# Pacing the first loads of the down projection at one per unit, starting them in the last gate/up block and holding that block's two pairs back

## The chip, the cores and the metric

One core of one Trainium2 chip runs the whole kernel. The metric is the device time of one execution in microseconds (us); times are medians of several runs, and one further execution of the kernel was profiled.

## What is computed

The reference is one decoder layer on 512 tokens of 2048 channels: a norm, three token mixers side by side, an output projection and a residual, then a norm and a SwiGLU feed-forward part with a residual:

```python
x = x + mix @ w_out[l]
h2 = _rms_norm(x, norm2_g[l])
x = x + (jax.nn.silu(h2 @ w_gate[l]) * (h2 @ w_up[l])) @ w_down[l]
```

The hidden width of the feed-forward part is 5632 = 44 tiles of 128. The change touches the two large stages of this last line: gate/up and down. Inputs and outputs are float32.

## The kernel before

**Products.** Both stages use a two-by-two block scheme with seven products in place of eight (a Strassen-like scheme), and every float32 product is made of three matmuls of rounded halves: high by high, high by low, low by high. So a weight block becomes `wh` and `wl`, and the other operand is a tile of two halves in one of 73 slots of 128 x 512 (`N_SLOTS`, L50; helper `slot`, L138).

**Units.** The work is a list of weight blocks of up to 128 x 1024. One block is one *unit*: 12 matmuls of 512 columns, or 6 for a block of half the size. For each unit the program writes down, in this order: the sums of raw weights that are due (`sums_now`, L289, GpSimd), the evacuations (`run(evacs)`), `next_unit` (L293) and the matmuls. `next_unit` asks for at most two more raw weight loads (`pump`, L235, 0.5 MB each on SP's queue at L243, eight buffers) and splits the block that is used two units later (`split_up_to`, L257: ScalarE writes `wn` at L269 and `wh` at L270, VectorE writes `wl` at L271, each from three buffers). After the matmuls come the loads of other operands (`load_next`) and the late work (`run(extras)`). Each engine works its own list in order, and waits only where a buffer or an operand is not ready; SP issues every DMA named here.

**Gate/up** (`class Up`, L1166) has 11 blocks (`NBLOCKS`) of 28 units: first four channel pairs by seven products of two units, then the other four pairs. The operands `ops[q, j]` come from the output projection; the steps of its last channel pair are still due when the first block begins, and L1324 runs one such step (`ticks.tick`) a unit: casts on ScalarE (L1030), and differences and low halves on VectorE (L1022 to L1036). When a block is done, its result (`b{n}c`, stored at L1266 into a DRAM tile `bd`) is read back turned, as two `Pair`s (L1119). A pair takes 17 extras: two reads of four 64 KB pieces (L1131), GpSimd sums (L1144 to L1149), seven pieces split by ScalarE (L1112) and GpSimd (L1116) and stored at L1101 into DRAM tiles `od`, from which the down stage reads its operands. L1241 puts the two pairs of a block at 5 and 18 extras after its end.

**Down** (`class Down`, L1361) has twelve steps t = 0 to 11, two for each of six ranges of pairs (`RANGES`: 4, 3, 4, 3, 4, 4 pairs). A step has seven products of two units, 14 units; with four pairs every unit has 12 matmuls, with three the second unit of a product has 6. I number the units of down from 0 (step t begins at unit 14t) and those of the last gate/up block from -28 to -1, and write "unit 6 of a step" for a place in it. Steps 2 and 3 work on the second range (pairs 4 to 6).

**The feed** (L1298 to L1316) is a fixed list of 170 loads of 256 KB: operands `a` (L1316) of the first range in the order of the products, mixed with the residuals `y` (L1311), of which eight belong to step 0 and eight to step 1; then the ranges that follow. I number the loads from 0: 0 to 35 belong to step 0, 36 to 43 are the residuals of step 1, 44 to 64 the operands of steps 2 and 3, 65 to 92 those of steps 4 and 5. `load_next(n, limit)` asks for the next n of them. Before the change it is asked for two in each unit of the second half of the last gate/up block (28 loads in units -14 to -1), two in each unit of step 0 (units 0 to 13), and one in each unit afterwards, as long as fewer than 46 operands are held (`FEED`).

The lines that set the pace:

```python
if n == NBLOCKS - 1 and blk.first:
    load_next(2)
...
load_next(2 if self.t == 0 else 1, FEED)
...
later(5 + 13 * at, Pair, self.dram, 2 * self.n + at, at, queue=extras)
```

Of the kernel before, what the change touches and what calls it, by code (L numbers as in the profile page):

```python
# [70 lines left out]
FEED = 46  # L71
NBLOCKS = NP // 2
# [44 lines left out]
def kernel(ctx: ExitStack, tc: tile.TileContext, xT, wi, wo, wgu, wd, cst_in, outT):  # L117
# [18 lines left out]
    ticks = Ticks()  # L136

    def slot(name, dt=F32, cols=T):  # L138
        return sp.tile([P, cols], dt, name=name, tag="s")
# [66 lines left out]
    for t, (g, r) in enumerate(DOWN):  # L206
        first, end = RANGES[r]
# [25 lines left out]
    at = {"entry": 0, "split": 0, "use": 0}  # L233
# [55 lines left out]
    def sums_now():  # L289
        for fn in sums.pop(at["use"], ()):  # L290
            fn()
# [143 lines left out]
    for k in range(KT):  # L435
# [5 lines left out]
        if k == 0:  # L441

            at["use"] = 2
            first = [splits.pop(u) for u in range(2)]
# [15 lines left out]
        if k == 0:  # L460
# [5 lines left out]
            first = w = None  # L466
# [613 lines left out]
    def norm2():  # L1080

        b = psum["high"].tile([P, 1024], F32, name="r2s", tag="h")[:, :NT]
        n2["r"] = token_scale(ssum2, D, "n2", b)[1]
# [3 lines left out]
    evacs, extras = [], []  # L1087
# [10 lines left out]
    def run(queue):  # L1098

        for fn, *args in queue.pop(0) if queue else ():  # L1100
            fn(*args)  # L1101

    def later(n, fn, *args, queue=evacs):
        while len(queue) <= n:
            queue.append([])
        queue[n].append((fn, *args))
# [59 lines left out]
    class Up:  # L1166
# [4 lines left out]
        def product(self, q):  # L1171
            banks = outs[:2]
            outs[:] = outs[2:] + banks
            for c in range(2):
                sums_now()
                run(evacs)
                wh, wl = next_unit()
                for a, b in enumerate(banks):
                    high, low = slice(a * P, (a + 1) * P), slice(TH + a * P, TH + (a + 1) * P)
                    for f in range(2):  # L1180
                        x, s = ops[q, self.first + 2 * c + f], slice(f * T, (f + 1) * T)
                        nc.tensor.matmul(b, x[:, high], wh[:, s], start=c == f == 0 and q in (7, 1, 5, 2), stop=False,  # L1182
                                         skip_group_check=True)
                        nc.tensor.matmul(b, x[:, high], wl[:, s], start=False, stop=False, skip_group_check=True)  # L1184
                        nc.tensor.matmul(b, x[:, low], wh[:, s], start=False, stop=c == f == 1, skip_group_check=True)  # L1185
                yield
                run(extras)
            later(0, self.done, self.first == 0, q, banks)
# [21 lines left out]
        def done(self, first, q, banks):  # L1210
            if first and q == 7:
                self.c = {}
            by = self.keep if first else self.add
            for a, b in enumerate(banks):
                if q == 7:
                    by(1, 1, a, b)
                elif q == 1:
                    by(0, 0, a, b)
                elif q == 4:
                    by(1, 0, a, b)  # L1220
                elif q == 6:
                    by(0, 1, a, b)
                    self.less(0, a, b)
                    self.less(1, a, b)
                elif q == 5:
                    self.less(1, a, b)
                else:
                    self.add(0, q - 2, a, b)
            if first:
                return  # L1230
            if q in (6, 5):
                later(1, self.gate, 6 - q, queue=extras)
            elif q == 2:
                self.dram = tc.dram_tile([T, T], F32, name=f"bd{self.n}")
            if q in (2, 3):
                later(0, self.weigh, q - 2)
                later(2, self.turn, q - 2)
                later(3, self.store, q - 2, queue=extras)
            if q == 3:
                for at in range(2):  # L1240
                    later(5 + 13 * at, Pair, self.dram, 2 * self.n + at, at, queue=extras)  # L1241

        def scale(self, k, a):
            i = 2 * k + a
# [41 lines left out]
    def turn_x2(key):  # L1286

        z = turns[key] = slot("z")
        for part in range(4):
            nc.sync.dma_start(by_blocks(z, part), turned(x2d, key, part))  # L1290
# [14 lines left out]
    def load_next(n, limit=99):  # L1305
        while feed and n and len(acts) < limit:
            key = feed.pop(0)
            n -= 1
            if len(key) == 4:
                y[key] = slot("y")  # L1310
                nc.sync.dma_start(y[key], x2t[key])  # L1311
            else:
                q, j = key
                acts[key] = slot(f"a{q}_{j}", F32R)
                at = LAID.index(q)
                nc.sync.dma_start(acts[key].bitcast(F32), od[j][:, at * T:(at + 1) * T])  # L1316

    for n in range(NBLOCKS):
        blk = Up(n)
        for blk.first in (0, 4):  # L1320
            for i, q in enumerate(ORDER):
                for c, _ in enumerate(blk.product(q)):
                    at_unit = (7 if blk.first else 0) * 2 + 2 * i + c
                    if ticks.due:  # L1324
                        ticks.tick()
                    if n == 0 and at_unit == 12:
                        norm2()
                    if 1 <= n <= 8 and at_unit in (9, 23):
                        key = SUMS[2 * n - 2 + at_unit // 16]
                        turn_x2(key)  # L1330
                        later(6, turn_x2_now, key)
                    if n == NBLOCKS - 1 and blk.first:
                        load_next(2)
                if n == NBLOCKS - 1:
                    for j in range(4):
                        ops.pop((q, blk.first + j))
# [24 lines left out]
    class Down:  # L1361
# [10 lines left out]
        def product(self, k, q):  # L1372
            banks = outs[:2]
            outs[:] = outs[2:] + banks
            tail = self.end and k == 6
            units = []
            for c in range(2):
                sums_now()
                run(evacs)
                units.append((next_unit(), list(enumerate(self.pairs[2 * c:2 * c + 2]))))  # L1380
                if not tail:
                    for a in range(2):
                        self.multiply(q, banks[a], units[c:], a, 0, T, c == 0, c == 1)
                    load_next(2 if self.t == 0 else 1, FEED)
                    run(extras)
            if tail:

                out = banks + outs[:1]
                sides = psum["high"].tile([P, 2, T], F32, name="sides", tag="h")
                last = [slot(f"end{c}")[:, :TH].rearrange("p (b a j) -> p b a j", a=2, j=32) for c in range(2)]  # L1390

                def turn(a):

                    src = y[self.sum(0, 1, a)]
                    for c in range(2):
                        nc.tensor.transpose(sides[:, c, a * P:(a + 1) * P], src[:, TH + c * P:TH + (c + 1) * P], ident)
                    for c in range(2):
                        eng, copy = ((nc.vector, nc.vector.tensor_copy), (nc.scalar, nc.scalar.copy))[c if a else 1]
                        copy(last[c][:, :, a], sides[:, c, a * P:(a + 1) * P].rearrange("p (b j) -> p b j", j=32))

                for n, (a, lo, hi) in enumerate(((0, 0, T), (1, 0, TH), (1, TH, T))):
                    if n == 2:
                        turn(0)
                    self.multiply(q, out[n], units, a, lo, hi, True, True)
                    if n == 0:
                        for b in range(2):
                            turn_back(self.sum(0, 0, b))
                        put(self.g, 0, 0)
                    t = y[self.sum(0, 1, a)][:, lo:hi]
                    nc.vector.tensor_add(t, t, out[n][:, lo:hi])  # L1410
                    if n < 2:
                        turn_back(self.sum(0, 1, a), 0, TH)
                    if n == 1:
                        put(self.g, 0, 1, 0, TH)
                turn(1)
                for c in range(2):
                    to = 512 * self.g + TH + c * P
                    nc.sync.dma_start(outT.rearrange("n p t -> (n p) t")[to:to + P, TH:], last[c].rearrange("p b a j -> p (b a j)"))
                return
            if self.drops:  # L1420
                for j in self.pairs:
                    acts.pop((q, j))
            later(0, self.done, q, banks)
# [64 lines left out]
    for t in range(len(DOWN)):  # L1488
        blk = Down(t)
# [87 lines left out]
```

## Time and profile before

| what | before |
|---|---|
| median of 3 runs | 1869.19 us (1866.34 to 1869.68) |
| the profiled execution's own time | 1867.57 us |
| its span, first to last instruction | 1865.7 us |
| granted TensorE clock, mean | 0.999 |
| first gate/up matmul, first and last down matmul | 581.7, 1422.4 and 1860.4 us |

The profile's page gives busy time by engine, the span in 40 slices, the chain of work that ended last, and groups of instructions. Further views give waits (who waited for whom), stretches of the span (busy time, number of instructions, granted clock and DMA share in each), and instructions in order of time. PE is TensorE, DVE VectorE, ACT ScalarE, POOL GpSimd; a trailing q is an engine's sequencer. The time between a DMA's issue and its landing is its landing time.

### The profile page before, as it was taken

Reading aid. Unit: us, or ns where it says so; the run is one execution under the profiler, and the core shown is the slowest. Engines: PE = TensorE matmul, PEld = TensorE weight load, DVE = VectorE, ACT = ScalarE, POOL = GpSimd, SP = SyncE. Lnnn points to the kernel's source line nnn. Section 1 sums busy time; section 2 is a strip of 40 time slices with the busy share of each in tenths; the row PEclk is TensorE's granted clock in tenths of the full one; section 3 lists DMA queues with packets and bytes.
Section 4 is the critical chain, followed back from the end, with each engine's and each line's share of the span. In section 5 each row is a group of like instructions: output and inputs, shape, how many; then the busy total and the mean of one; then the engine's idle time right before and its main releaser. Section 6 shows DMA issues by size and latency. Waiting matters only on the chain.

```text
span 1865.7 us, 26613 instructions
## 1 busy us (share of the span) xinstructions
PE 1844.3 (99%) x8370; PEld 1527.3 (82%) x8370; DVE 1432.0 (77%) x2052; ACT 1321.4 (71%) x1794; POOL 1103.0 (59%) x850
## 2 busy tenths in 40 slices
PE   9999999999999999999999999999999899999999
PEld 7888888888887888888888888888888677888887
DVE  6778878998689777777777777777777477777777
ACT  6355644553458788888888888878888577778775
POOL 0135533100003567777787877867877799879775
PEclk9999999999999999999999999999999999999999
DMA  7242253343343366777776876777679887566545
GB/s 273 83 140 92 77 146 97 92 131 119 133 139 107 103 164 177 206 213 177 220 196 189 220 198 185 221 183 218 175 227 285 277 269 268 197 222 234 178 140 113
DMA packets 382988, 330.36 MB, mean 177 GB/s; under 512 B 171648, under 2 KB 311552, under 8 KB 382848
## 3 DMA queue, kind: packets, MB, share of 16 engines
q1 hardware_dynamic: 382704, 328.66, 59.6%
q8 instruction: 66, 1.08, 0.2%
q14 instruction: 74, 0.61, 0.1%
q10 hardware_dynamic: 144, 0.01, 0.0%
HBM read 255.56 MB, written 64.63 MB: 172 GB/s over the span
## 4 chain that ended last, share of the span: by engine, by line
PE 92%; DMA 3%; POOL 2%; DVE 1%; issue 1%; ACT 1%; SPq 0%; POOLq 0%; DVEq 0%; ACTq 0%
PE out L1184 15%; PE out L1182 15%; PE out L1185 15%; PE out L1432 6%; PE out L1431 6%; PE out L1433 6%; PE o L310 3%; PE o L308 3%; PE o L309 3%; PE cq L308 2%; PE cq L309 2%; PE cq L310 2%; PE ak L308 1%; PE aq L308 1%; PE av L308 1%
## 5 line engine op out<-in xcount | busy, mean ns | idle before, releaser
L1184 PE MATMUL out<-wl,h 128*128 128x512 f32 x1232 | 479.4, 389 | 1.6 <-DVE wl L271 1.6
L1182 PE MATMUL out<-wh,h 128*128 128x512 f32 x1232 | 479.4, 389 | 0.0
L1185 PE MATMUL out<-wh,h 128*128 128x512 f32 x1232 | 479.3, 389 | 0.0
L1184 PEld LDWEIGHTS out<-wl,h 128*128 128x128 f32 x1232 | 231.3, 188 | 50.0 <-DVE wl L271 2.0
L1185 PEld LDWEIGHTS out<-wh,h 128*128 128x128 f32 x1232 | 231.3, 188 | 48.0
L1182 PEld LDWEIGHTS out<-wh,h 128*128 128x128 f32 x1232 | 231.3, 188 | 47.8
L1431 PE MATMUL out<-wh,a 128*128 128x512 f32 x620 | 242.0, 390 | 11.6 <-ACT wh L270 11.6
L1432 PE MATMUL out<-wl,a 128*128 128x512 f32 x620 | 242.0, 390 | 1.7 <-DVE wl L271 1.6
L1433 PE MATMUL out<-wh,a 128*128 128x512 f32 x620 | 241.1, 389 | 0.0
L275 ACT CAST wh<-w 128x1024 fp32r<-128x1024 f32 (+2 forms) x94 | 96.9, 1031 | 154.2 <-PE o L309 64.8
L1431 PEld LDWEIGHTS out<-wh,a 128*128 128x128 f32 x620 | 116.8, 188 | 39.0 <-ACT wh L270 15.1
L253 DVE TENSOR_TENSOR wl<-w,wh 128x1024 fp32r<-128x1024 f32 (+2 forms) x95 | 113.1, 1191 | 42.3 <-ACT wh L275 40.8
L1432 PEld LDWEIGHTS out<-wl,a 128*128 128x128 f32 x620 | 116.7, 188 | 27.6 <-DVE wl L271 3.3
L1433 PEld LDWEIGHTS out<-wh,a 128*128 128x128 f32 x620 | 116.9, 189 | 23.6
L1441 DVE TENSOR_TENSOR y<-y,out 128x512 f32<-128x512 f32 x164 | 106.1, 683 | 22.5 <-PE out L1433 20.8
L519 DVE SCALAR_TENSOR_TENSOR y<-bu,cst,y 128x511 f32<-128x511 f32 (+14 forms) x120 | 89.9, 749 | 0.7
L308 PE MATMUL o<-mh_c,wh 128*128 128x512 f32 x128 | 51.1, 399 | 0.0
L308 PE MATMUL cq<-hh,wh 128*128 128x512 f32 x128 | 50.5, 395 | 0.0
L310 PE MATMUL o<-mh_c,wl 128*128 128x512 f32 x128 | 50.0, 391 | 0.0
L309 PE MATMUL cq<-hl,wh 128*128 128x512 f32 x128 | 49.9, 390 | 0.0
L309 PE MATMUL o<-ml_c,wh 128*128 128x512 f32 x128 | 49.9, 390 | 0.0
L310 PE MATMUL cq<-hh,wl 128*128 128x512 f32 x128 | 49.9, 390 | 0.0
(2376 smaller groups left out, 4877.4 us busy)
## 6 DMA issues: line engine op xcount, KB each, us to landing
od<-a SPq DMA_DIRECT2D x154, 256.0 KB, 4.1
a<-od SPq DMA_DIRECT2D x154, 256.0 KB, 6.0
w<-in_wi SPq DMA_DIRECT2D x58, 512.0 KB, 3.3
w<-in_wo SPq DMA_DIRECT2D x32, 512.0 KB, 3.3
x<-in_xT SPq DMA_DIRECT2D x16, 256.0 KB, 6.9
xr<-in_xT SPq DMA_DIRECT2D x16, 256.0 KB, 3.6
x2d<-xr SPq DMA_DIRECT2D x16, 256.0 KB, 2.0
z<-x2d SPq DMA_DIRECT2D x64, 64.0 KB, 4.1
```

What stands on the lines that cost most here:

```text
L253: fn(*args)
L275: (nc.vector.tensor_copy if u == 0 else nc.scalar.copy)(hi[:, :n], t[:, :n])
L308: nc.tensor.matmul(out, wh, xh, start=start, stop=False)
L309: nc.tensor.matmul(out, wh, xl, start=False, stop=False)
L310: nc.tensor.matmul(out, wl, xh, start=False, stop=stop)
L1182: nc.tensor.matmul(b, x[:, high], wh[:, s], start=c == f == 0 and q in (7, 1, 5, 2), stop=False, skip_group_check=True)
L1184: nc.tensor.matmul(b, x[:, high], wl[:, s], start=False, stop=False, skip_group_check=True)
L1185: nc.tensor.matmul(b, x[:, low], wh[:, s], start=False, stop=c == f == 1, skip_group_check=True)
L1431: nc.tensor.matmul(b[:, lo:hi], x[:, high], wh[:, s], start=start, stop=False, skip_group_check=True)
L1432: nc.tensor.matmul(b[:, lo:hi], x[:, high], wl[:, s], start=False, stop=False, skip_group_check=True)
L1433: nc.tensor.matmul(b[:, lo:hi], x[:, low], wh[:, s], start=False, stop=last, skip_group_check=True)
L1441: getattr(eng, op)(t, t, src)
```

## The change

Three edits, in gate/up and down:

- The two pairs of the last gate/up block start 25 and 45 extras after its end, not 5 and 18.
- The feed is asked for one load a unit throughout: 24 loads in units -24 to -1 (all units of the last block but its first four), and one in each unit of step 0 as well.
- The steps of the last channel pair run in every second unit (the odd ones) of the first gate/up block.

```diff
             if q == 3:
+                first, every = (25, 20) if self.n == NBLOCKS - 1 else (5, 13)
                 for at in range(2):
-                    later(5 + 13 * at, Pair, self.dram, 2 * self.n + at, at, queue=extras)
+                    later(first + every * at, Pair, self.dram, 2 * self.n + at, at, queue=extras)
...
-                    if ticks.due:
+                    if ticks.due and at_unit % 2:
                         ticks.tick()
...
-                    if n == NBLOCKS - 1 and blk.first:
-                        load_next(2)
+                    if n == NBLOCKS - 1 and at_unit > 3:
+                        load_next(1)
...
-                    load_next(2 if self.t == 0 else 1, FEED)
+                    load_next(1, FEED)
```

## The prediction

> **What bounds the kernel now.** The page comes first. TensorE is the bound, and the chain of work that ended last is 92% PE, so only TensorE's idle time can be gained.
>
> ```profile
> span 1865.7 us, 26613 instructions
> PE 1844.3 (99%) x8370; PEld 1527.3 (82%) x8370; DVE 1432.0 (77%) x2052; ACT 1321.4 (71%) x1794; POOL 1103.0 (59%) x850
> ...
> PE 92%; DMA 3%; POOL 2%; DVE 1%; issue 1%; ACT 1%; SPq 0%; POOLq 0%; DVEq 0%; ACTq 0%
> ```
>
> The view by stretches shows where it idles. The numbers after x are matmuls: 443 in an undisturbed 100 us, one per 0.227 us.
>
> ```profile
> 500.00:600.00 100.00, 98.39 (x435) 81.17 (x434) 84.21 (x142) 65.99 (x120) 15.18 (x7) 1.00 0.38 126
> ...
> 1400.00:1500.00 100.00, 90.93 (x384) 72.17 (x383) 64.33 (x76) 70.96 (x89) 73.55 (x54) 0.98 0.88 281
> 1500.00:1600.00 100.00, 95.74 (x419) 78.00 (x418) 72.34 (x91) 75.49 (x98) 92.46 (x66) 1.00 0.81 267
> 1600.00:1700.00 100.00, 100.00 (x443) 82.84 (x442) 74.22 (x93) 75.09 (x92) 78.14 (x49) 1.00 0.63 204
> ```
>
> 59 + 24 matmuls are missing after 1400, that is 83 x 0.227 = **18.8 us**, and 8 before 600, **1.8 us**: 20.6 us to be had. The waits of PE name who ended them, and the order in time shows the worst.
>
> ```profile
> PE out L1431 <- ACT wh L270: 11.6, 8, 2.7
> PE out L1184 <- DVE wl L271: 1.6, 1, 1.6
> PE out L1432 <- DVE wl L271: 1.6, 3, 0.7
> ```
>
> ```profile
> 1467.26 0.50 PE L1431 MATMUL out<-wh,a 128*128 128x512 f32 x1 [2.73 <-ACT wh L270]
> ...
> 1469.24 0.63 PE L1431 MATMUL out<-wh,a 128*128 128x512 f32 x1
> 1469.67 0.63 PE L1432 MATMUL out<-wl,a 128*128 128x512 f32 x1
> ...
> 1491.88 0.50 PE L1431 MATMUL out<-wh,a 128*128 128x512 f32 x1 [1.72 <-ACT wh L270]
> ...
> 1545.79 0.50 PE L1431 MATMUL out<-wh,a 128*128 128x512 f32 x1 [1.42 <-ACT wh L270]
> ```
>
> After the idle time of 2.73 us matmuls start 0.43 us apart, not 0.227, for eight of them: a second price of about 1.65 us. After 1.72 us idle nothing of the kind shows. So an idle time of 2.7 us costs 4.4.
>
> Why was `wh` late? SP, POOL and ACT in order of time, before that first long wait (unit 15):
>
> ```profile
> 1453.27 4.55 SPq L1131 DMA_DIRECT2D p20l<-bd  x4
> 1457.93 1.44 SPq L243 DMA_DIRECT2D w('11', 'd1B')_14171<-in_wd  x1
> ```
>
> ```profile
> 1462.81 2.38 POOL L172 TENSOR_TENSOR w('s', 'd1B')_14277<-w('21', 'd1B')_14137,w('11', 'd1B')_14171 128x1024 f32<-128x1024 f32 x1 [4.73 <-DMA w('11', 'd1B')_14171<-in_wd]
> ```
>
> ```profile
> 1465.22 1.02 ACT L269 CAST wn<-w('s', 'd1B')_14277 128x1024 fp32r<-128x1024 f32 x1 [5.10 <-POOL w('s', 'd1B')_14277 L172]
> ```
>
> The weight was asked for only at 1457.93, behind the reads of pair 20, and POOL then idled 4.73 us for it. The DMA side was full there: the second half of the last gate/up block, step 0, and for comparison step 6 of down (the last two numbers are DMA share and GB/s).
>
> ```profile
> 1384.30:1422.40 38.10, 38.10 (x170) 31.56 (x169) 28.71 (x32) 32.09 (x39) 25.73 (x20) 1.00 0.93 284
> 1422.40:1460.90 38.50, 37.97 (x166) 30.66 (x165) 27.22 (x32) 27.67 (x34) 31.92 (x24) 1.00 0.89 301
> 1650.70:1679.30 28.60, 28.60 (x128) 23.68 (x127) 22.64 (x30) 21.82 (x30) 22.66 (x15) 1.00 0.66 208
> ```
>
> **The change part by part.** *Steps of the last channel pair.* The short stall near 594 is VectorE's: the low halves and differences of that pair stand in front of a `wl`, and one of them takes 2.63 us.
>
> ```profile
> 587.95 2.63 DVE L1036 TENSOR_TENSOR h<-tb,h 128x256 fp32r<-128x256 f32 x1
> ...
> 593.35 1.21 DVE L271 TENSOR_TENSOR wl<-w('22', 'u0A')_5725,wn 128x1024 fp32r<-128x1024 f32 x1
> ```
>
> Four steps are left when gate/up begins; they go from units 0 to 3 to units 1, 3, 5 and 7. Their results are read from unit 14 on and the sum of squares at unit 12, so nothing waits for them. I take the whole 1.8 us; the bounds are 0 and 1.8.
>
> *Fewer loads in step 0, pairs moved.* Step 0 loses 14 loads of 256 KB (3.7 MB of the 11.6 MB that 38.5 us at 301 GB/s make) and steps 0 and 1 lose the reads of pairs 20 and 21, so the rate falls to some 205 GB/s, that of step 6, which has no stall. In units -14 to -1 the same 14 loads go. Ten loads appear in units -24 to -15, 2.6 MB in 27 us, hidden by weights that come two units ahead; bounds 0 and 1. What stays is POOL's work in step 0:
>
> ```profile
> 1427.59 0.74 POOL L1144 TENSOR_TENSOR p19a<-p19l 128x256 f32<-128x256 f32 x1
> ...
> 1432.29 2.54 POOL L1257 TENSOR_TENSOR b10c<-b10c,b10c 128x512 f32<-128x512 f32 x2
> ...
> 1439.50 1.43 POOL L1116 TENSOR_TENSOR a<-p19r,a 128x256 fp32r<-128x256 f32 x2
> ...
> 1442.99 2.56 POOL L1441 TENSOR_TENSOR y<-y,d0u 128x512 f32<-128x512 f32 x2
> ```
>
> Eight weight sums of 2.4 us (19.2), four products of the last block (5.1), pair 19 with four sums of 0.74 and seven pieces of 0.72 (8.0) and eight residual sums of 1.28 (10.2) are 42.5 us for a step of 38. The small waits of step 0 (before 1467) are its share; I leave 0.8 us. **Saved: 18.8 + 1.8 - 0.8 = 19.8 us.**
>
> *What is late next: the loads themselves.* This is the term that decides. At one a unit the feed runs close to its use. By unit 28, where step 2 begins, 24 + 28 = 52 loads have been asked for: the 44 of steps 0 and 1 and 8 of step 2. Step 2 eats three in two units and gets two. So its last loads are asked for hardly ahead: with full units of 2.72 us and half ones of 1.36, load 55 is asked for 8.2 us before its matmul, 58 6.8, 59 5.4, 60 4.8, 61 4.1, 62 4.1, 63 2.0 and 64 2.7 us. In step 0 load 35 has 6.1 us, in step 4 loads 90 to 92 have 6.1, 5.4 and 3.4 us.
>
> How long does a load take from its unit's start? Step 6 has the same half units and one load a unit. It begins with the matmul at 1650.71, so its units 3 to 12 start at 1657.5, 1658.9, 1661.6, 1663.0, 1665.7, 1667.0, 1669.8, 1671.1, 1673.8 and 1675.2.
>
> ```profile
> 1650.71 0.39 PE L1431 MATMUL out<-wh,a 128*128 128x512 f32 x1
> ```
>
> ```profile
> 1660.49 1.54 SPq L1316 DMA_DIRECT2D a<-od  x3
> 1666.35 0.38 SPq L243 DMA_DIRECT2D w('11', 'd7A')_16143<-in_wd  x1
> ...
> 1667.38 1.22 SPq L1316 DMA_DIRECT2D a<-od  x1
> ...
> 1669.17 1.41 SPq L1316 DMA_DIRECT2D a<-od  x3
> 1673.20 0.38 SPq L243 DMA_DIRECT2D w('22', 'd7A')_16227<-in_wd  x1
> 1673.67 0.46 SPq L1316 DMA_DIRECT2D a<-od  x1
> ...
> 1675.21 2.49 SPq L1316 DMA_DIRECT2D a<-od  x5
> ```
>
> ```profile
> L1316 SPq DMA_DIRECT2D a<-od x10: 382/422/1215, 1667.4 to 1677.2; - x10
> ...
> DMA to landing us min/median/max: 4.6/5.4/6.4
> ```
>
> SP is held by the weight loads, which wait for a buffer that VectorE frees. So the operand loads go out 3.0, 2.2 and 0 us after the start of units 3 to 5, then 4.4 (unit 6), 3.5, 2.7 and 0.4 (units 7 to 9), 2.6 (10), 1.4 and 0.6 (11, 12). With the median landing of 5.4 us load 55 (unit 3) is there after 8.4 us, 0.2 late. Load 58 (unit 6) comes after 9.8 against 6.8 + 0.2: 2.8 late, before unit 37. Load 59: 8.9 against 5.4 + 0.2 + 2.8, 0.5 late. Loads 60 and 61 are covered by that. Load 62 (unit 10): 8.0 against 4.1 + 0.5, 3.4 late; load 63: 6.8 against 2.0 + 3.4, 1.4 late; load 64 is covered. Sum in step 2: **8.3 us**. Two of these idle times are near or over 2.73, so I add 1.65 twice: **3.3 us**. Bounds by the extremes of landing, 4.6 and 6.4: 5 and 13 us together.
>
> Step 0 and step 4 have full units. Step 5 shows SP there:
>
> ```profile
> 1642.39 0.46 SPq L1316 DMA_DIRECT2D a<-od  x1
> ...
> 1644.32 2.39 SPq L1316 DMA_DIRECT2D a<-od  x5
> ```
>
> Units 10 and 11 of step 5 start at 1639.8 and 1642.6, so the loads go 2.6 and 1.8 us after, and land 5 us later: load 35 after 6.8 against 6.1, **0.7 us**; load 90 after 7.6 against 6.1, **1.5 us**, which covers 91 and 92. The residuals of step 1 stop VectorE, not PE: load 43 is asked for 2.7 us before its sums, lands 5.4 to 6.9 us after its unit's start, and a `wl` stands behind the sums; VectorE is two units ahead, which leaves 0 to 1, taken as **0.5 us**. Paid: 8.3 + 3.3 + 0.7 + 1.5 + 0.5 = **14.3 us**.
>
> *Pairs 20 and 21 at their new place.* Reads at units 26, 28, 46 and 48 meet SP when it has no weights to ask for. Their 8.0 us of POOL work each come at units 35 to 42 and 55 to 64; the first falls on a step where POOL is busy 22.7 of 28.6 us, but beside the stalls just counted, so it costs nothing; without those stalls it would cost some 2 us.
>
> A page to weigh. The Trainium skill, "TensorE: Matmul & The Clock Gate", section "Why this matters for your kernels", asks for no PE idle gap over some 3 us, as one idle window halves the clock. The trace halves it after 2.73 us already; by the page's bound only the idle time of 3.4 us would pay and the sum would be 1.65 us lower.
>
> **Sum.** -19.8 + 14.3 = -5.5 us: 1867.6 - 5.5 = 1862.1 against the profiled execution's own time (span 1865.7 and 1.9 around it). The median of the runs shown is 1869.2, which gives 1863.7. I predict **1862.9 us**, halfway.
>
> **The rivals.** *The loads come sooner (0.22).* With a thinner queue a load lands in 4 us or less, 1.5 us sooner than taken. Then only loads 58 to 63 are late, by 5.4 us with one slow stretch of 1.65: paid 7, saved 19.8, so about 1855. For it: landings of step 0 before, in a full queue, are no measure. Against: step 6 is not full and has 5.4. The Trainium skill, "DMA: Bandwidth & Descriptors", section "Anatomy of one DMA — SWDGE (gpsimd) path", gives some 2.0 us and the bytes by 436 GB/s; an estimate by it is 2.6 us for 256 KB, and the time would fall to about 1852. No load in the rows above lands so fast.
>
> *The loads come later: slower (0.18).* Each microsecond of landing or of SP's lag is paid at six places one after another (units 13, 22, 37, 38, 40, 68), so 6 us for one. The gain is gone at 0.9 us later; at 2 us later, from pair 20's reads and stores on the same queue or from a weight load that waits for POOL, 14.3 + 12 - 19.8 = +6.5, about 1875. For it: SP's queue is in order. Against: in steps 2 to 4 the pairs bring few bytes.
>
> *The old stalls stay in part (0.13).* If POOL's 42.5 us for 38 in step 0, not the DMA, made `wh` late, half of the 18.8 stay, partly beside the new waits: about 1868. Against: POOL idled 4.73 us for a DMA just before.
>
> **How the numbers follow.** The forecast has 0.47 (1858 to 1868). A measurement of this kernel can tell about 0.2% from no change, 3.7 us. Faster: 0.34 of the forecast, 0.22 and 0.02 of the last rival, 0.58; same: 0.13 + 0.09 + 0.03, 0.25; slower 0.17. The range runs from the sooner loads, 1855, to 1.2 us later ones, 1871.
>
> **What would show it.** Right: no wait for `wh` between 1420 and 1500; DMA share of step 0 near 0.65; PE waiting for DMA `a<-od` at units 37 to 40 with 3 us and a half clock after it; smaller such waits at units 13 and 68. Wrong: PE still waits for ACT in step 1, or no wait for `a`, or waits of 5 us and more at units 13 and 68.

## The result, and the profile after

| | before | after |
|---|---|---|
| median | 1868.81 us (11 runs, 1865.40 to 1872.25) | 1872.51 us (11 runs, 1868.52 to 1877.69) |
| ratio, with its 95% interval | | 1.0022 (1.0011 to 1.0032) |
| span of the profiled execution | 1865.7 us | 1870.6 us |

The kernel became slower, by 2 to 6 us: 0.1 to 0.3%, small but clear of the noise, as the interval leaves out 1. 6 us faster were forecast. The stretches of the span after the change show where TensorE stands still now (the first numbers of a row are the stretch and PE's busy time, x its matmuls).

```profile
500.00:600.00 100.00, 100.00 (x443) 82.81 (x442) 82.18 (x137) 65.57 (x119) 16.02 (x7) 1.00 0.42 132
...
1400.00:1500.00 100.00, 96.06 (x421) 78.48 (x421) 72.20 (x84) 77.03 (x90) 82.10 (x56) 1.00 0.74 243
1500.00:1600.00 100.00, 90.94 (x384) 72.47 (x383) 65.65 (x83) 70.76 (x98) 82.34 (x63) 0.97 0.71 222
1600.00:1700.00 100.00, 96.83 (x418) 79.01 (x417) 69.85 (x87) 70.65 (x87) 79.36 (x50) 0.98 0.66 221
```

The gap near 594 is gone (443 matmuls). After 1400, 22 + 59 + 25 = 106 matmuls are missing, 24.1 us, where 83 were missing before: 15 more than the 91 of before in all, or 3.4 us. The rest of the 4.9 us between the spans lies outside: gate/up began 1.9 us later in this one execution, and the profiled executions of the ten kernels below, none of which changes anything ahead of it, put that start anywhere from 581.5 to 583.4.

The waits are others now. PE's waits in steps 0 and 1, in step 2 and in step 4 of down (three windows of the view of waits; total us, times, longest):

```profile
PE out L1432 <- DMA a<-od: 3.9, 2, 2.2
```

```profile
PE out L1432 <- DMA a<-od: 5.0, 3, 2.2
PE out L1432 <- ACT wn L269: 1.6, 1, 1.6
```

```profile
PE out L1432 <- DMA a<-od: 3.2, 3, 2.4
PE out L1432 <- ACT wh L270: 1.9, 2, 1.5
PE out L1433 <- DVE wl L271: 0.5, 1, 0.5
```

Before, ACT and DVE ended every wait there, because of weights; now it is mostly the loads of the feed. (L1432 to L1434 are the three matmuls of down; the diff moved them by a line.) Added up by unit, as the excess of the matmuls' start-to-start times over 0.227 us (matmuls at half clock included), the profiled executions give:

| waits in us | steps 0, 1 (units 0 to 27) | steps 2, 3 (28 to 55) | step 4 (56 to 69) | all |
|---|---|---|---|---|
| before | 13.3 | 5.5 | 0 | 18.9 |
| after | 4.9 (units 11, 13, 22) | 10.1 (35 to 40) | 9.0 (57 to 69) | 23.9 |
| pairs alone | 4.1 | 1.2 | 6.4 | 11.7 |
| feed alone | 7.6 | 12.1 | 1.9 | 21.7 |
| two loads a unit in step 0 | 0.8 | 1.2 | 4.8 | 6.7 |
| the same, pair 21 at 59 | 1.5 | 1.2 | 0 | 3.0 |

("All" counts step 5 too: 0.3 us in the last row. Such a sum makes each wait some 0.2 us longer than the view of waits does.)

The 9.0 us of step 4 are of two kinds: 3.4 at units 57, 63 and 64 are waits for weights, 5.7 at units 66 to 69 are waits for loads of the feed and the half clock behind one of them.

The worst place is unit 40, in order of time on PE:

```profile
1533.51 0.77 PE L1432 MATMUL out<-wh,a 128*128 128x512 f32 x1 [2.21 <-DMA a<-od]
1534.07 0.63 PE L1433 MATMUL out<-wl,a 128*128 128x512 f32 x1
...
1536.93 0.80 PE L1432 MATMUL out<-wh,a 128*128 128x512 f32 x1 [1.80 <-DMA a<-od]
1537.53 0.63 PE L1433 MATMUL out<-wl,a 128*128 128x512 f32 x1
...
1539.66 0.61 PE L1432 MATMUL out<-wh,a 128*128 128x512 f32 x1
1540.09 0.42 PE L1433 MATMUL out<-wl,a 128*128 128x512 f32 x1
1540.34 0.39 PE L1434 MATMUL out<-wh,a 128*128 128x512 f32 x1
```

It waits 2.21 us for load 62, works three matmuls, waits 1.80 for load 63, and all matmuls up to 1540 start 0.43 us apart. SP shows why the loads are late:

```profile
1528.95 0.38 SPq L243 DMA_DIRECT2D w('22', 'd3A')_14879<-in_wd  x1
1529.43 0.45 SPq L1317 DMA_DIRECT2D a<-od  x1
1530.68 0.38 SPq L243 DMA_DIRECT2D w('22', 'd3B')_14907<-in_wd  x1
1531.12 0.50 SPq L1317 DMA_DIRECT2D a<-od  x1
```

Load 62 goes out at 1529.43, behind the weight load of its unit, and lands at 1533.4; load 63 goes out at 1531.12, 1.3 us after its unit's start (1529.8), lands 5.8 us later, at 1536.9, and had been due at 1534.2.

The prediction had named one more sign: a DMA share near 0.65 and some 205 GB/s in step 0. It did not come. The stretch of step 0 after the change (the last two numbers are DMA share and GB/s):

```profile
1422.30:1460.40 38.10, 35.93 (x159) 29.35 (x158) 27.57 (x33) 28.95 (x36) 37.67 (x28) 1.00 0.81 285
```

Before, SP had issued only 21 loads of the feed in these 38 us, of the 28 that step 0 asks for. After the change it issued 14: 7 fewer, not 14, and 8 weight loads and 7 stores of pieces in place of 6 and 4.

### The profile page after: what moved, and what is told of

Same layout as the page of the kernel before. It is cut to its first block, busy times and chain, and to the rows that moved or that the text cites. A ratio compares the mean times of both kernels' runs of the same rounds, so it can differ in the third digit from the quotient of the medians.

```text
span 1870.6 us, 26605 instructions
## 1 busy us (share of the span) xinstructions
PE 1846.8 (99%) x8370; PEld 1528.0 (82%) x8370; DVE 1432.9 (77%) x2052; ACT 1322.3 (71%) x1794; POOL 1106.7 (59%) x850
## 4 chain that ended last, share of the span: by engine, by line
PE 93%; DMA 4%; POOL 1%; ACT 1%; issue 0%; SPq 0%; DVE 0%; POOLq 0%; ACTq 0%; DVEq 0%
PE out L1184 15%; PE out L1182 15%; PE out L1185 15%; PE out L1432 6%; PE out L1433 6%; PE out L1434 6%; PE o L310 3%; PE o L309 3%; PE o L308 3%; DMA a<-od 2%; PE cq L308 1%; PE cq L309 1%; PE cq L310 1%; PE ak L308 1%; PE aq L308 1%; PE av L308 1%
## 5 line engine op out<-in xcount | busy, mean ns | idle before, releaser
L1432 PE MATMUL out<-wh,a 128*128 128x512 f32 x620 | 243.5, 393 | 15.7 <-DMA a<-od 12.1
L1434 PE MATMUL out<-wh,a 128*128 128x512 f32 x620 | 241.8, 390 | 0.0
L1432 PEld LDWEIGHTS out<-wh,a 128*128 128x128 f32 x620 | 117.2, 189 | 44.8 <-DMA a<-od 10.7
L1434 PEld LDWEIGHTS out<-wh,a 128*128 128x128 f32 x620 | 117.3, 189 | 24.4
```

Source lines behind the costliest of these rows:

```text
L1432: nc.tensor.matmul(b[:, lo:hi], x[:, high], wh[:, s], start=start, stop=False, skip_group_check=True)
L1434: nc.tensor.matmul(b[:, lo:hi], x[:, low], wh[:, s], start=False, stop=last, skip_group_check=True)
```

## Experiments

Every kernel is compared with before; all ratios lie between 0.990 and 1.003, and the 95% interval says which of them are clear of the noise. Waits are those of one profiled execution. Theory A: the loss is operand loads that come late because the feed runs at one a unit. Theory B, the rival: the loss is the pairs' work in their new place, on GpSimd and SP.

**The steps of the last channel pair alone**

```diff
-                    if ticks.due:
+                    if ticks.due and at_unit % 2:
```

> Only the steps of the last channel pair in every second unit; feed and pairs as before. Both theories: the one short wait of gate/up is gone (1.9 us at its 12th to 14th us), nothing else moves: about 2 us less than before. If the loss of the whole change came from here, the time would be over before's.

1865.91 us against 1867.78, ratio 0.9990 (0.9980 to 0.9999). The wait of gate/up is gone, the waits of down are as before (19.8 us). This edit does what it seems to, and the loss is not here.

**The pairs alone**

```diff
+                first, every = (25, 20) if self.n == NBLOCKS - 1 else (5, 13)
...
-                    later(5 + 13 * at, Pair, ...
+                    later(first + every * at, Pair, ...
```

> Only the last block's pairs later (25 and 45); feed two a unit as before. Theory A (the loss is operand loads that come late because the feed runs at one a unit): loads are far ahead here, so PE waits for no a<-od; the weight of step 1 no longer queues behind pair 20's reads, so the old waits of units 15 to 42 (18 us) shrink to 6 to 12: 6 to 12 us less than before. Theory B (the loss is GpSimd's and SP's work for the pairs in their new place): PE waits for ScalarE with 5 us and more in units 56 to 66, and the time is within 3 us of before.

1861.89 us against 1867.78, 0.9967 (0.9956 to 0.9979). PE waits for no load of the feed:

```profile
PE out L1432 <- ACT wh L270: 5.0, 3, 3.5
PE out L1433 <- DVE wl L271: 2.2, 5, 0.9
```

Of the 18.9 us, 13.6 go, though the feed still asks for two a unit and step 0's DMA share is 0.91. But 6.4 us of new waits for weights stand in step 4, units 57 to 64: the number that theory B named for this place. Both theories have a part.

**The feed alone**

```diff
-                    if n == NBLOCKS - 1 and blk.first:
-                        load_next(2)
+                    if n == NBLOCKS - 1 and at_unit > 3:
+                        load_next(1)
...
-                    load_next(2 if self.t == 0 else 1, FEED)
+                    load_next(1, FEED)
```

> Only the feed at one a unit from the fifth unit of the last gate/up block; pairs at 5 and 18 as before. Theory A: the waits for a<-od stay near units 11 to 13 and 37 to 40 and grow, as the reads and stores of pairs 20 and 21 now share steps 0 to 2 with them: 15 to 25 us of waits, 0 to 8 us more than before; step 4's waits (9 us in the changed kernel) shrink to 1 or 2. Theory B: with the pairs back in place the waits fall to 10 us, 8 us less than before.

1872.93 us against 1867.78, 1.0029 (1.0016 to 1.0041). Nearly all old waits for weights are gone with the pairs at their old place, and 21.7 us stand there instead, nearly all for loads:

```profile
PE out L1431 <- DMA a<-od: 13.7, 8, 3.0
PE out L1432 <- DVE wl L271: 0.4, 1, 0.4
```

(Of the other 7.6 us some 5 are matmuls at half clock after three of these waits, eight each at 0.2 us too much; the rest is the 0.2 us by which the sum counts each wait longer.) So the pairs alone and the feed alone each remove the same old waits, 13.6 and 18.9 us, which can be saved only once; each brings its own new ones, 6.4 and 21.7 us. In step 4 these add up (6.4 and 1.9 make 9.0), in steps 0 to 3 the feed's 19.7 us are 15.0 with the pairs gone from there: 23.9 us together, against a sum of 28.1. That is why edits of -0.10, -0.33 and +0.29% make +0.22% together.

**The changed kernel with two loads a unit in step 0**

```diff
-                    load_next(1, FEED)
+                    load_next(2 if self.t == 0 else 1, FEED)
```

> The changed kernel, but step 0 asks for two loads a unit as before the change (the last gate/up block still for 24 at one a unit). Theory A: each later load has 14 units more, so no wait for a<-od in steps 2 and 4 (19 us in the changed kernel) and fewer in step 0; step 0's DMA share goes back to 0.9, some waits for weights return: 10 to 15 us less than before. Theory B: the 9 us of step 4 stay, as pair 21 stays where it is: 3 to 6 us less than before.

1856.50 us against 1867.78, 0.9943 (0.9926 to 0.9959). No wait for the feed is left:

```profile
PE out L1432 <- ACT wh L270: 3.3, 2, 1.7
PE out L1433 <- DVE wl L271: 1.9, 3, 0.9
```

Step 0 has no wait though its DMA share is 0.86 and 299 GB/s; 0.8 us stand at unit 22. Theory A holds for steps 0 and 2. In step 4, 4.8 us for weights stay (units 57, 63, 64). The profiled execution was the fastest of four, at 1853.10, and the median is 3.4 us above it: other executions lose more than these waits show.

**Pair 21 out of step 4**

```diff
-                first, every = (25, 20) if self.n == NBLOCKS - 1 else (5, 13)
+                first, every = (25, 34) if self.n == NBLOCKS - 1 else (5, 13)
```

> The changed kernel with pair 21 14 units later (59 extras after the block, its GpSimd work in step 5). Theory C: GpSimd has no room for pair 21's 8 us at the start of step 4, so the weights and with them SP's loads come 5 to 10 us late there; its 9.0 us of waits in units 57 to 69 fall to 1 to 2 (what the feed alone left in step 4), steps 0 and 2 keep their 15 us: about 7 us less than the changed kernel, 1865. Rival D: step 4's waits come from the one-a-unit feed alone: 6 us or more stay, 1870 or more.

1865.83 us against 1868.22, 0.9987 (0.9978 to 0.9997). Step 4's waits fall from 9.0 to 2.8 us, and those for weights go entirely, while steps 0 to 3 have 17.5 in this execution (15.0 in the changed kernel). In the changed kernel GpSimd looked like this at the start of step 4 (order in time; step 4 begins at 1570.5):

```profile
1569.24 2.39 POOL L172 TENSOR_TENSOR w('s', 'd4B')_15220<-w('21', 'd4B')_15117,w('11', 'd4B')_15145 128x1024 f32<-128x1024 f32 x1 [3.60 <-DMA w('11', 'd4B')_15145<-in_wd]
1571.58 2.55 POOL L1442 TENSOR_TENSOR y<-y,d3u 128x512 f32<-128x512 f32 x2
1574.08 0.74 POOL L1144 TENSOR_TENSOR p21a<-p21l 128x256 f32<-128x256 f32 x1
...
1586.04 1.44 POOL L1116 TENSOR_TENSOR a<-p21r,a 128x256 fp32r<-128x256 f32 x2
1587.43 2.39 POOL L172 TENSOR_TENSOR w('11', 'd4B')_15145<-w('21', 'd4B')_15117,w('11', 'd4B')_15145 128x1024 f32<-128x1024 f32 x1
```

and SP behind it, by its waits and in order of time:

```profile
SPq L243 <- DVE wl L271: 10.1, 2, 9.9
SPq L243 <- POOL w('11', 'd4B')_15145 L172: 5.2, 1, 5.2
```

```profile
1583.60 0.38 SPq L243 DMA_DIRECT2D w('12', 'd4A')_15343<-in_wd  x1
1584.03 0.50 SPq L1317 DMA_DIRECT2D a<-od  x1
1589.85 0.38 SPq L243 DMA_DIRECT2D w('12', 'd4B')_15370<-in_wd  x1
1590.28 0.51 SPq L243 DMA_DIRECT2D w('21', 'd5A')_15372<-in_wd  x1
1590.83 0.50 SPq L1317 DMA_DIRECT2D a<-od  x1
...
1597.31 0.77 SPq L1317 DMA_DIRECT2D a<-od  x1
```

```profile
1604.27 0.50 PE L1432 MATMUL out<-wh,a 128*128 128x512 f32 x1 [2.38 <-DMA a<-od]
```

GpSimd has no idle time from 1569 to 1606. Pair 21 stands among its sums, a weight load waits 5.2 us for one of them, and the operand load behind that goes out at 1590.83, 11.5 us after its unit (59, at 1579.3) began. In step 6 before, the same place of a step had 3.0 us. The load that PE then waits 2.38 us for is a later one: asked for in unit 62 (at 1587.5), issued at 1597.31, 9.8 us after its unit began, landed at 1604.2. With pair 21 in step 5 the loads of units 59 and 62 go out 5.2 and 4.2 us after their units.

Why step 5 can bear the pair shows in the stretches: GpSimd was busy 45.0 us in step 4 with the pair there, for a step that lasts 38 undisturbed, and 35.4 with most of the pair moved on; in step 5 it was busy 27.1 us before the move and 33.4 after it. Theory C holds: the pair's work alone costs 4.8 to 6.4 us there, by weights that come late, where the feed has a lead; the feed alone costs 1.9; together they cost 9.0, as the pair's work also delays SP and the feed has no lead to bear it.

**Two loads a unit in step 1**

```diff
-                    load_next(1, FEED)
+                    load_next(2 if self.t == 1 else 1, FEED)
```

> The changed kernel with two loads a unit in step 1 (14 loads more by its end), one in step 0. Feed theory: step 0's 4.6 us (units 11 and 13) stay, step 2's 10.1 us are gone, in step 4 the waits for a<-od (5 to 6 us) go and those for ScalarE (3.4) stay: 8 us of waits, 15 us less than the changed kernel, about 1857. Rival: the fuller queue of step 1 brings waits for weights there, over 5 us.

1858.19 us against 1868.22, 0.9949 (0.9934 to 0.9965). Step 2 has no wait, step 0 keeps 2.5 us, step 4 keeps its waits for weights, which now come to 6.3 us with the slow matmuls after one of 3.3 us:

```profile
PE out L1432 <- ACT wh L270: 3.3, 1, 3.3
PE out L1432 <- DMA a<-od: 1.9, 2, 1.7
PE out L1433 <- DVE wl L271: 1.7, 2, 1.2
```

As the feed theory said, 14 loads of lead, asked for in step 0 or in step 1, are enough for the feed in steps 2 and 4. Up to the end of step 0 this kernel is the changed one, and yet its step 0 waited 2.5 us, not 4.6 (5.4 with pair 21 out of step 4): what step 0 costs differs by that much between executions.

**Pair 19 out of step 0: what makes SP late there?**

```diff
-                first, every = (25, 20) if self.n == NBLOCKS - 1 else (5, 13)
+                first, every = (25, 20) if self.n == NBLOCKS - 1 else (5, 30) if self.n == NBLOCKS - 2 else (5, 13)
```

> The changed kernel with pair 19 (of the block before the last) 17 extras later, so that its GpSimd work falls in step 1, not step 0. Theory E: in step 0 GpSimd has 42.5 us of work for 38, the weight loads that wait for its sums hold SP back, and the operand loads behind them go out 4 to 7 us after their unit instead of 0 to 3: with pair 19 gone the lag of units 2 to 8 falls by 3 us or more and the 4.6 us of waits at units 11 and 13 shrink to under 1; up to 3 us may come back in step 1. Rival F: the loads are late by their landing (6 to 8 us there), not by SP's lag: the 4.6 us stay over 3.

1871.51 us against 1868.22, 1.0019 (1.0009 to 1.0030). It did not decide (the profiled execution is the slowest of the ten, at 1874.69): the loads of units 2 to 5 go out 3.2, 3.4, 2.2 and 0.0 us after their units, not 7.1, 7.3, 6.1 and 5.7, and the wait at unit 11 is gone, but 2.25 us stay at unit 13. SP shows that the experiment had put something of its own before load 35:

```profile
1450.70 0.46 SPq L1317 DMA_DIRECT2D a<-od  x1
1451.21 2.29 SPq L1131 DMA_DIRECT2D p19r<-bd  x4
1453.61 0.91 SPq L243 DMA_DIRECT2D w('22', 'd1B')_14212<-in_wd  x1
1454.61 0.45 SPq L1317 DMA_DIRECT2D a<-od  x1
```

So pair 19 went further, with `(5, 36)` in place of `(5, 30)`:

> The changed kernel with pair 19 23 extras later (its reads at units 14 and 16, its GpSimd work at units 23 to 32), so neither its sums nor its reads stand in step 0. With pair 19 17 extras later SP's lag in units 2 to 8 fell from 5.7 to 2.4 us, but the reads of pair 19 then stood right before load 35 and 2.25 us stayed at unit 13. Theory E (lag by GpSimd's work and by SP's own queue): under 1 us left at units 11 to 13. Rival F (landing of 6 to 8 us): 2 us or more left there. In the steps behind, pair 19 meets pair 20 in steps 1 and 2, which costs 0 to 6 us more; the time itself, 1866 to 1874, decides nothing.

1873.35 us against 1867.97, 1.0030 (1.0019 to 1.0040); 0.6 us is left at unit 13 and nothing at unit 11, though the operand loads of units 7 to 9 still take 6.4 to 7.5 us to land. SP there:

```profile
1450.04 0.38 SPq L243 DMA_DIRECT2D w('22', 'd1A')_14178<-in_wd  x1
1450.48 0.50 SPq L1317 DMA_DIRECT2D a<-od  x1
1452.02 0.38 SPq L243 DMA_DIRECT2D w('22', 'd1B')_14202<-in_wd  x1
1452.49 0.46 SPq L1317 DMA_DIRECT2D a<-od  x1
```

The loads of units 10 and 11 go 2.5 and 1.8 us after their units (1448.0 and 1450.7), the 2.6 and 1.8 of step 5 before. By its waits theory E holds. But this does not rule out the landing, for with pair 19's work its transfers left step 0 too, whose DMA share is 0.72 here. The two loads that PE waited for in the changed kernel, 31 (for unit 11) and 35 (for unit 13):

| | load 31: issued after its unit began, landed after its issue | load 35 | wait at units 11 and 13 |
|---|---|---|---|
| changed kernel | 5.7, 8.2 | 3.7, 6.8 | 2.5, 2.1 |
| two loads in step 1 (the same step 0) | 3.4, 8.5 | 1.8, 6.7 | 0.5, 2.0 |
| pair 19 17 extras later | 2.3, 6.1 | 4.0, 4.2 | 0, 2.25 |
| pair 19 23 extras later | 2.3, 6.4 | 1.8, 4.7 | 0, 0.6 |

The second row has load 35 issued as early as the last, and PE still waits 2.0 us for it, for its landing of 6.7 us. At unit 11 the first two rows differ by the issue alone, and by 2 us of wait. So both SP's lag and a landing of 6 to 8 us have a part in step 0, and pair 19 bears on both; how much of either is its GpSimd work and how much its transfers stays open. The time did not fall with these waits because steps 2 to 4 waited more in these two executions (24.9 and 23.1 us, 19.1 in the changed kernel); why is not shown.

**The best of them: two loads a unit in step 0, pair 21 at 59**

```diff
-                first, every = (25, 20) if self.n == NBLOCKS - 1 else (5, 13)
+                first, every = (25, 34) if self.n == NBLOCKS - 1 else (5, 13)
...
-                    load_next(1, FEED)
+                    load_next(2 if self.t == 0 else 1, FEED)
```

> Two loads a unit in step 0 as before the change, pair 21 at 59, the rest as changed. If theory C holds, the 4.8 us of waits at units 57, 63 and 64 that the kernel with two loads in step 0 still had go as well: 1 to 3 us of waits left in all, 1851 to 1853. Rival: pair 21 only moves its waits to step 5: within 1 us of that kernel, 1856.

1849.63 us against 1868.22, 0.9902 (0.9883 to 0.9921): 15 to 22 us less than before, faster than both kernels.

```profile
PE out L1433 <- DVE wl L271: 1.4, 2, 0.9
PE out L1432 <- ACT wh L270: 0.3, 1, 0.3
```

**Before with the pairs alone at 25 and 59**

```diff
+                first, every = (25, 34) if self.n == NBLOCKS - 1 else (5, 13)
...
-                    later(5 + 13 * at, Pair, ...
+                    later(first + every * at, Pair, ...
```

> Before with the pairs alone at 25 and 59; feed and channel steps as before. If step 4's waits of the kernel with pairs at 25 and 45 (6.4 us in units 57 to 64) are pair 21's GpSimd work, they go, and 5 us stay in steps 0 to 3: 1861.9 - 6.4 = 1855 to 1856. If the feed of two a unit was as bad as the pairs' place, waits of 10 us and more stay: 1860 or more.

1855.32 us against 1867.97, 0.9930 (0.9913 to 0.9946). The waits of step 4 go; 5.3 us stay in steps 0 and 1, and 1.2 in step 3. The kernel before this one has 1.5 in steps 0 and 1; of the two edits that it has more, only the earlier and slower start of the feed in the last gate/up block bears on them, the other belongs to gate/up. Most of what there was to gain, 12.7 of 18.6 us, is the place of two pairs.

## Why the prediction was wrong

- *Step 4* is where the sum broke. The prediction took 1.5 us, for load 90 alone, with SP's lag read from step 5, where GpSimd has less to do; of pairs 20 and 21 at their new place it said "so it costs nothing". 9.0 us were measured. The prediction had weighed pair 20's 8 us of GpSimd work against step 2 and not done the same for pair 21 in step 4, where GpSimd was busy 45.0 us with it for a step of 38, after a first sum that had waited 3.60 us for its weight. So weights came late (3.4 us at units 57, 63, 64), and the loads of units 58 to 65 went out 3.8 to 11.5 us after their units (5.7 us at units 66 to 69). With pair 21 in step 5, 2.8 us were left, and 1.9 with the feed alone: the feed's own share had been sized well.
- *Step 0* was mis-sized. 0.8 us for GpSimd's overload and 0.7 for load 35 were forecast, 4.6 measured. The overload (42.5 us for 38) had been counted, but only for the weights; that SP's queue passes it on to the loads behind a weight was left out (loads 31 and 35 went out 5.7 and 3.7 us after their units, where 1.8 was taken for load 35). And the queue was thought thin, 205 GB/s, with a landing of 5 us; it moved 285 GB/s, and the two loads took 8.2 and 6.8 us to land. Without pair 19 there, 0.6 us was left. Whether the late issue or the long landing weighs more stays open.
- *What is saved* was right in size. The old waits of down (18.8 us) and the one of gate/up (1.8 us) are gone. That DMA made the weights late was right; but the cause given, a rate that falls to 205 GB/s, did not come about, and with the pairs alone moved 13.6 us went at a DMA share of 0.91. Those waits needed both pair 20's reads and the feed at two a unit, and taking away either is enough for most of them; that was not seen.
- *Step 2* was right in its mechanism and near in its total. 8.3 + 3.3 = 11.6 us were forecast, 10.1 measured, at units 35 to 40, with the half clock behind the last of them; the loads of units 38 and 39 went out 2.5 and 1.3 us after their units (forecast 2.6 and 1.4). That the total came so near is in part luck, as the parts differ: idle times of 2.21 and 1.80 us at unit 40, not 3.4 and 1.4, and one half-clock stretch of 6.83 us, not two of 3.41. The wait at unit 37, 1.64 us, is put down to ScalarE, but its load 58 had landed only 0.1 us earlier.
- *Unit 22*: 0.5 forecast, 0.3 measured.
- Sum: -20.6 + 24.1 = +3.5 us by the profiled executions (3.4 when counted in matmuls). Against the forecast 7.5 us were added in step 4 and 3.1 in step 0, and 1.7 taken off in step 2 and at unit 22. What came is in the main the rival "the loads come later", with the cause it named ("a weight load that waits for POOL"); it had 0.18. But the lag was not the same 2 us at six places: against the forecast it was 1 to 2 us more in units 10 and 11 of step 0, up to 8 more in step 4, none in step 2, and 3.4 us of step 4 are waits for weights, which that rival did not have.

## What to carry to other kernels

When loads are asked for at fixed places of a program, compare the rate with the use over the hungriest stretch: three operands in two units against one a unit used up a lead of eight loads within one step and ended with a load asked for 2 us before its use; 14 loads more of lead were enough. SP works its list in order and hands every delay on to what stands behind it, so work given to an engine that has no room for it in that stage (45.0 us for a step of 38) is paid by loads that have nothing to do with it; look which waits stand ahead of them in the queue. And two edits that remove the same wait save it once, but each brings its own new wait.

## What had not been expected of the hardware

The clock halved after shorter idle times than the 2.73 us of before. The stretches of after around units 13, 40 and 66 (the last three numbers: granted clock, DMA share, GB/s):

```profile
1460.00:1470.00 10.00, 8.23 (x37) 6.51 (x36) 5.76 (x7) 5.90 (x6) 7.19 (x4) 1.00 0.40 143
1530.00:1540.00 10.00, 5.99 (x16) 4.07 (x15) 3.01 (x4) 3.61 (x6) 8.43 (x8) 0.66 0.95 332
...
1600.00:1610.00 10.00, 7.62 (x27) 5.80 (x26) 4.28 (x6) 4.59 (x5) 10.00 (x8) 0.83 1.07 381
```

An idle time of 2.17 us at 1455 and one of 1.77 at 1462 left the clock whole; 2.38 us at 1604 halved it for 3.41 us. At unit 40 it fell at 1533.3, at the end of the idle time of 2.21 us, and stayed low for 6.83 us, twice that; the idle time of 1.80 three matmuls later fell into this stretch. In other kernels 2.32 us (pairs alone at 25 and 59) and 2.42 us (pair 19 further out) left it whole. And in the kernel with pair 21 out of step 4 an idle time of 2.00 us that ended at 1521.6 left it whole, and another of 2.00 us, ended at 1534.5, halved it. So the length alone does not decide.

The traces' records of the clock show what does. In each trace all changes of the clock lie whole multiples of 3.413 us apart: in the changed kernel at 1533.29, 1540.11, 1604.97 and 1608.38, which are 2, 19 and 1 times that. Cut at these points into intervals of 3.413 us, from 600 to 1800 us, the twelve traces of this case agree: each of the 15 intervals at full clock with 1.99 us or more of PE idle time in it is followed by one at half clock, and no interval with 1.79 us or less is.

| idle time of PE, us | most idle time in one interval, us | clock after it |
|---|---|---|
| 2.32 (pairs alone at 25 and 59) | 1.43 | whole |
| 2.17 (changed kernel, 1455) | 1.75 | whole |
| 2.42 (pair 19 further out) | 1.79 | whole |
| 2.21 (changed kernel, unit 40) | 1.99 | half |
| 2.00 (pair 21 out of step 4, 1534) | 2.00 | half |
| 2.38 (changed kernel, 1604) | 2.38 | half |

The Trainium skill, "TensorE: Matmul & The Clock Gate", section "Why this matters for your kernels", draws the line at some 3 us of idle; in these runs 2.00 us were enough where they fell into one interval, and 2.42 us split over two were not. A wait that halves the clock costs its own length and about 1.7 us more for an interval at half clock that is filled with matmuls.
